# First adaLN scale in quarters, and the first projections by quarters of k, in a hybrid decoder step

## The chip, the core and the metric

The kernel runs on one core of one Trainium2 chip. It is one launch. The metric is the time of that launch on the device in microseconds (us), the median of several runs. The engines are TensorE (PE), VectorE (DVE), ScalarE (ACT), GpSimd (POOL) and SyncE (SP). SP issues nearly all of the loads.

## What is computed

One layer of a decoder runs over 256 prompt tokens and 8 samples of 4 tokens: 288 columns in all. What matters here is its beginning:

```python
mod = jax.nn.silu(c) @ P['w_ada'] + P['b_ada']          # 9 conditions, 2048 x 12288
sh1, sc1, gt1, sh2, sc2, gt2 = split(mod, 6)
xn = rmsnorm(x, P['g_norm1']) * (1.0 + sc1) + sh1
proj = xn @ P['w_in']                                   # 2048 x 12312
```

The parts of `proj` then feed an RG-LRU branch, a GLA branch and an mLSTM branch, whose merged output, with a gate, is added to x. A squared-ReLU MLP with its own scale and shift follows, and a last RMSNorm. All inputs are f32. The outputs are y and the branches' new states.

## The kernel before

Activations lie feature by feature: a k-tile is 128 features on the partitions by 288 columns (256 of the prompt, 32 of the samples). x has 16 k-tiles and fills two buffers, `xa` and `xb`; there are ten such buffers of eight k-tiles, `slot(0)` to `slot(9)`.

**Projections.** `stream` runs through the weights by blocks of 512 output features and, inside a block, by groups of two k-tiles. A group is one DMA of 512 KB into `raw`; ACT rounds it to `hi` (L156), DVE makes the rest `lo` (L157). Each matmul of f32 precision is three in the faster type: hi times xh (L163), hi times xl (L164), lo times xh (L165), where xh and xl are the same two parts of the activation (`split`, L431 and L432). A group is 24 matmuls. There are three buffers each of `raw`, `hi` and `lo`. A block's results leave PSUM by ACT (`to_slot`) or, if they are added to an earlier part, by DVE (`plus_slot`, L470).

**Conditioning.** `cond_product` multiplies silu(c) with one kind of `w_ada`, load by load (1 MB each), in matmuls whose output is 32 partitions wide (L256); four such column groups of PE take the four 32-feature parts of the columns. At the end `by_feature` transposes the result on DVE (L219), and `ada_finish` adds the bias (L278, L281). `units` gives the order of these loads: first scale in two halves (`sc0`, `sc`), first shift, then a correction, then the other kinds.

**The early projections.** The first three blocks (`NPRE`; the q, k and part of v) start before the shift is known: they take the scaled norm without shift, and the correction `shift_product`, shift times weights, is added later. They run over the first eight k-tiles as soon as `sc0` is there, then over the other eight. Then the shift is added to the activations (`shift`; `whole` first rebuilds them from xh and xl on POOL), and all later blocks use the full ones.

**Order.** The code gives the order of the SP queue by hand. `every` sets a pattern, one word for each weight group: L issues one conditioning load, V multiplies those that have landed. `slots` lists the buffers that conditioning loads take in turn (L, in five buffers, during the early projections). The order of the instructions on PE, ACT, DVE and POOL is made by a planner when the program is built; each engine then works through its list in that order.

## Time and profile before

| | |
|---|---|
| median of 3 runs | 2000.64 us (2000.48 to 2002.02) |
| the profiled execution | 1999.18 us, of which the profile's span is 1997.4 us |
| PE busy in the span | 1960.1 us (98%) |
| DVE, ACT, POOL busy | 1018.1, 820.3, 250.2 us |
| first projection matmul | at 38.32 us |
| end of the last product of the first shift | at 131.88 us |
| first projection matmul with shifted activations | at 143.81 us |

Times in the profile count from the start of the span. A row of a group gives the line, the engine, the operation, the output and inputs by the program's names, and how often it ran. In a row of the timeline or of the chain the first number is the start and the second the length. A matmul's length is modelled; the distance between two starts tells the rate. A row of waits says who waited, for whom, and then the total, the number and the longest wait. A row of a stretch gives each engine's busy time and number of instructions, then PE's granted clock (1.00 is full), the busy share of the DMA engines, and GB/s.

### The profile page before, as it was taken

To read this page: it belongs to the slowest core of one execution; us is meant where nothing else is said; L and a number is where in the kernel's file an instruction comes from. 1 tells how busy PE (TensorE), PEld (TensorE's weight loads), DVE (VectorE), ACT (ScalarE), POOL (GpSimd) and SP (SyncE) were. 2 spreads that over 40 slices of the span, in tenths; PEclk is the share of its full clock that TensorE was granted. 3 is DMA by queue.
4 is the path that set the end of the run, shared out by engine and by line. 5 is a ranking of instruction groups with operands and counts; after the bars stand their busy time and mean duration, and the time that the engine had idled before them with its cause. 6 is when DMAs were issued, how large, how long until landed. Compare 5 with 4: busy or idle time off the path is not lost.

```text
span 1997.4 us, 35369 instructions
## 1 busy us (share of the span) xinstructions
PE 1960.1 (98%) x14830; PEld 1839.4 (92%) x14830; DVE 1018.1 (51%) x1496; ACT 820.3 (41%) x1153; POOL 250.2 (13%) x330
## 2 busy tenths in 40 slices
PE   6999999999999999999999999999999999999997
PEld 4879888998899998899999989999999999999997
DVE  3453556545673456554444564334454545444565
ACT  3333465535454344343333454443343434343433
POOL 0300200001124021200112331000000101010101
PEclk8999999999999999999999999999999999999999
DMA  9988755647644358967779646654445444444443
GB/s 373 399 331 289 284 211 220 243 149 245 201 152 137 124 174 261 311 219 267 265 274 353 249 134 225 221 201 159 158 166 174 166 161 159 171 167 169 159 159 121
DMA packets 119472, 429.56 MB, mean 215 GB/s; under 512 B 11760, under 2 KB 11920, under 8 KB 119184
## 3 DMA queue, kind: packets, MB, share of 16 engines
q1 hardware_dynamic: 109744, 392.56, 54.9%
q0 software_dynamic: 7984, 28.99, 4.3%
q10 hardware_dynamic: 1584, 5.75, 0.8%
q8 instruction: 116, 1.90, 0.4%
q14 instruction: 44, 0.36, 0.1%
HBM read 410.44 MB, written 16.81 MB: 214 GB/s over the span
## 4 chain that ended last, share of the span: by engine, by line
PE 93%; DMA 4%; DVE 2%; issue 0%; ACT 0%; POOL 0%; DVEq 0%; ACTq 0%; SPq 0%; POOLq 0%
PE mm L163 28%; PE mm L165 27%; PE mm L164 27%; PE pa L256 5%; DMA s<-wada 1%; DMA o_C_s<-st 1%; DVE s L537 1%; DMA s<-x 1%; DVE lo L157 0%; DMA st<-mC 0%; PE px L586 0%; PE px L817 0%; DMA o_C_s<-s 0%; PE px L1197 0%; PE pi L1262 0%
## 5 line engine op out<-in xcount | busy, mean ns | idle before, releaser
L157 DVE TENSOR_TENSOR lo<-raw,hi 128x1024 fp32r<-128x1024 f32 x450 | 558.2, 1242 | 611.8 <-ACT hi L156 583.2
L156 ACT ACTIVATE hi<-raw 128x1024 fp32r<-128x1024 f32 x450 | 476.8, 1060 | 833.9 <-PE mm L164 601.1
L163 PE MATMUL mm<-xh,hi 128*128 128x288 f32 x2576 | 763.6, 300 | 6.8 <-ACT xh L431 4.6
L164 PE MATMUL mm<-xl,hi 128*128 128x288 f32 x2576 | 758.7, 297 | 0.0
L165 PE MATMUL mm<-xh,lo 128*128 128x288 f32 x2576 | 738.5, 296 | 1.7 <-DVE lo L157 1.7
L163 PEld LDWEIGHTS mm<-xh,hi 128*128 128x128 f32 x2576 | 483.8, 189 | 32.4 <-issue 14.5
L163 PE MATMUL mm<-s,hi 128*128 128x288 f32 x1664 | 490.6, 297 | 0.1
L164 PE MATMUL mm<-s,hi 128*128 128x288 f32 x1664 | 488.6, 295 | 0.0
L164 PEld LDWEIGHTS mm<-xl,hi 128*128 128x128 f32 x2576 | 486.1, 189 | 2.2 <-issue 0.5
L165 PEld LDWEIGHTS mm<-xh,lo 128*128 128x128 f32 x2576 | 478.9, 189 | 4.3 <-DVE lo L157 2.3
L165 PE MATMUL mm<-s,lo 128*128 128x288 f32 x1664 | 476.7, 295 | 0.4 <-DVE lo L157 0.4
L163 PEld LDWEIGHTS mm<-s,hi 128*128 128x128 f32 x1664 | 311.8, 188 | 5.7 <-issue 4.2
L164 PEld LDWEIGHTS mm<-s,hi 128*128 128x128 f32 x1664 | 312.5, 188 | 0.8 <-issue 0.5
L165 PEld LDWEIGHTS mm<-s,lo 128*128 128x128 f32 x1664 | 308.4, 188 | 2.1 <-issue 1.3
L157 DVE TENSOR_TENSOR lo<-s,hi 128x1024 fp32r<-128x1024 f32 x80 | 98.0, 1225 | 114.9 <-ACT hi L156 114.9
L156 ACT ACTIVATE hi<-s 128x1024 fp32r<-128x1024 f32 x80 | 84.9, 1062 | 142.8 <-PE mm L164 142.1
L1446 POOL TENSOR_TENSOR t<-t 128x288 f32<-128x288 f32 x64 | 60.2, 951 | 645.0 <-ACT t L1445 645.0
L256 PE MATMUL pa<-s,silc 128*32 128x512 f32 (+1 forms) x496 | 54.3, 523 | 6.0 <-DMA s<-wada 6.0
L1462 DVE TENSOR_TENSOR s<-s,mm 128x288 f32<-128x288 f32 x96 | 40.3, 450 | 33.9 <-PE mm L165 32.6
L969 POOL TENSOR_TENSOR s<-s,t 128x288 f32<-128x288 f32 x32 | 29.5, 948 | 193.4 <-DVE t L968 193.4
L432 DVE TENSOR_TENSOR s<-t,s 128x288 fp32r<-128x288 f32 x64 | 33.8, 568 | 15.6 <-ACT s L431 15.6
L256 PEld LDWEIGHTS pa<-s,silc 128*32 128x32 f32 x496 | 14.6, 112 | 27.1 <-issue 14.5
(379 smaller groups left out, 1148.2 us busy)
## 6 DMA issues: line engine op xcount, KB each, us to landing
raw<-win SPq DMA_DIRECT2D x192, 512.0 KB, 4.8
raw<-wf SPq DMA_DIRECT2D x176, 512.0 KB, 4.2
s<-wada SPq DMA_DIRECT2D x49, 1024.0 KB, 9.0
s<-wf SPq DMA_DIRECT2D x80, 512.0 KB, 3.5
ag<-wada SPq DMA_DIRECT2D x29, 1024.0 KB, 5.8
raw<-wout SPq DMA_DIRECT2D x32, 512.0 KB, 6.1
st<-wada SPq DMA_DIRECT2D x24, 512.0 KB, 6.9
s<-win SPq DMA_DIRECT2D x14, 768.0 KB, 6.6
```

What stands on the lines that cost most here:

```text
L156: pace["hi"] = S.activation(hi, raw, AF.Copy)
L157: pace["lo"] = V.tensor_tensor(out=lo, in0=raw, in1=hi.bitcast(F32), op=ALU.subtract)
L163: T.matmul(pss[m][:, :N], hi[:, kk, ms], xh, start=k == k0, stop=False)
L164: T.matmul(pss[m][:, :N], hi[:, kk, ms], xl, start=False, stop=False)
L165: pace["last"] = T.matmul(pss[m][:, :N], lo[:, kk, ms], xh, start=False, stop=k == kt - 1)
L256: pace["prod"] = T.matmul(ps[32 * j:32 * j + 32, h * w // 4:(h + 1) * w // 4], stat(k), v[:, j], start=k == 0 and h == 0, stop=k == KT - 1 ...
L432: V.tensor_tensor(out=dst_l[:, r], in0=src[:, r], in1=dst_h[:, r].bitcast(F32), op=ALU.subtract)
L537: V.scalar_tensor_tensor(y[:, m, s:NP], x[:, m, 0:NP - s], w[:, m, j:j + 1], y[:, m, s:NP], ALU.mult, ALU.add)
L969: G.tensor_tensor(out=a, in0=a, in1=t, op=ALU.add)
L1446: G.tensor_tensor(out=r, in0=r, in1=r, op=ALU.mult)
L1462: V.tensor_tensor(out=a, in0=a, in1=p, op=ALU.add)
```

## The change

- x is loaded on SP's queue right behind the conditions; before, it came on ACT's queue. The `eye` constants come early, the rest of the constants later.
- The squares of x are made by ACT and DVE in turn and summed in four column groups of PE; x is multiplied by the norm at once, in place.
- The first scale comes in quarters of 512 columns (four k-tiles of the activation). The first quarter goes through `cond_product`. The others (`ada_quarter`) give each of PE's four column groups another k-tile and all 512 columns, so that four partial sums arise; two copies on ACT and eight small matmuls with `eye` add and transpose them.
- The early projections run by quarters of k: three blocks over four k-tiles each, four times. The results of the second to fourth quarter are added on DVE. The first weight group is loaded and converted ahead (`fetch`), before the last load of the first quarter.
- Loads of the second and third quarter and the first of the shift are mixed by hand; eight buffers take them in turn.
- `modulate` scales or shifts x in place, on DVE alone; POOL's part and `whole` are gone. The shift of k-tiles 0 to 11 is applied when the shift's product ends, which is before the last early block; that of 12 to 15 after it.

```diff
...
         at["n"] += 1
         return [weight_tile(n) for n in ("raw", "hi", "lo")]
+    fetched = []
+    def fetch(w, blk, g, kg=2, ahead=True):
+        with tc.high_priority() if ahead else nullcontext():
+            raw, hi, lo = (t.rearrange("p (k m) -> p k m", k=kg) for t in weight_tiles())
+            Q.dma_start(raw, w[blk, g].rearrange("p (k m) -> p k m", k=kg))
+            pace["hi"] = S.activation(hi, raw, AF.Copy)
+            pace["lo"] = V.tensor_tensor(out=lo, in0=raw, in1=hi.bitcast(F32), op=ALU.subtract)
+        return hi, lo
     def stream(w, blk, act, kt, evac, g0=0, width=512, ahead=True, k0=0, kg=2):
         nm_t = width // P
         pss = [pm.tile([P, 512], F32, tag="mm", name=nm("mm")) for _ in range(nm_t)]
         for g in range(k0 // kg, kt // kg):
-            with tc.high_priority() if ahead else nullcontext():
-                raw, hi, lo = (t.rearrange("p (k m) -> p k m", k=kg) for t in weight_tiles())
-                Q.dma_start(raw, w[blk, g0 + g].rearrange("p (k m) -> p k m", k=kg))
-                pace["hi"] = S.activation(hi, raw, AF.Copy)
-                pace["lo"] = V.tensor_tensor(out=lo, in0=raw, in1=hi.bitcast(F32), op=ALU.subtract)
+            hi, lo = fetched.pop(0) if fetched else fetch(w, blk, g0 + g, kg, ahead)
             for m in range(nm_t):
                 for kk in range(kg):
                     k = kg * g + kk
...
             if next(g, side) is side:
                 side.remove(g)
+    def halves(a, b):
+        return lambda k: a[:, k, :] if k < 8 else b[:, k - 8, :]
     ct, th9 = (t288()[:, 0:KT * 9].rearrange("p (k c) -> p k c", k=KT) for _ in range(2))
     Q.dma_start(ct, io["ct"])
+    xa, xb = slot(0), slot(1)
+    xin = halves(xa, xb)
+    for i in range(4):
+        Q.dma_start((xa, xb)[i // 2][:, 4 * (i % 2):4 * (i % 2) + 4, :], io["x"][:, 4 * i:4 * i + 4, :])
+    a, w = COFF["eye"]
+    G.dma_start(con[:, a:a + w], io["con"][:, a:a + w])
     S.activation(th9, ct, AF.Tanh, scale=0.5)
+    S.activation(sc([P, 1], "warm", 1), th9[:, 0, 0:1], AF.Sqrt, bias=eps, scale=0.0)
     V.scalar_tensor_tensor(th9, th9, 1.0, ct, ALU.add, ALU.mult)
     silc = cp.tile([P, KT * 9 + 23], F32, tag="silc", name="silc")
     V.memset(silc[:, KT * 9:], 0.0)
...
             return [sp.tile([P, 1028], F32, tag="st", name=nm("st"), bufs=2)[:, 0:1024] for _ in range(2)]
         return [flat(slot(i))[:, 0:2048]]
-    def cond_product(name, load, each, cols, stat, finish):
+    def cond_product(name, load, each, cols, stat, finish, bank=None):
         acc_ = []
         def products(raw, q):
             if not acc_:
-                acc_.append(pa.tile([P, 512], F32, tag="pa", name=nm("pa")))
+                acc_.append(bank() if bank else pa.tile([P, 512], F32, tag="pa", name=nm("pa")))
             ps = acc_[0]
             w = cols // len(raw)
             for i in range(each):
...
         def end():
             hs = range(-(-cols // 1024))
-            with tc.high_priority():
-                pvs = [by_feature(acc_[0], h, min(256, cols // 4 - 256 * h)) for h in hs]
             for h in hs:
                 with tc.high_priority():
-                    finish(h, pvs[h])
+                    finish(h, by_feature(acc_[0], h, min(256, cols // 4 - 256 * h)))
         n = KT // each
         for q in range(n):
...
                     Q.dma_start(raw[h], wada[kind, h, k])
             else:
                 Q.dma_start(raw[0].rearrange("p (h m) -> p h m", h=2), wada[kind, :, k].rearrange("h p m -> p h m"))
+        def first_shift(h, pv):
+            ada_finish(kind)(h, pv)
+            for q in ((0, 1), (2,))[h]:
+                modulate(4 * q, ALU.add, kind, 2 if q else 1)
+        if kind == SH1:
+            return cond_product(kind, load, 1, 2048, silu_c, first_shift, longp)
         return cond_product(kind, load, 1, 2048, silu_c, ada_finish(kind))
-    def ada_half(name, kind, h):
+    def first_quarter(kind):
         def load(raw, q):
-            Q.dma_start(raw[0].rearrange("p (k m) -> p k m", k=2), wada[kind, h, 2 * q:2 * q + 2].rearrange("k p m -> p k m"))
-        return cond_product(name, load, 2, 1024, silu_c, lambda _, pv: ada_finish(kind)(h, pv))
+            Q.dma_start(raw[0].rearrange("p (k m) -> p k m", k=4), wada[kind, 0, 4 * q:4 * q + 4, :, 0:512].rearrange("k p m -> p k m"))
+        return cond_product("sc0", load, 4, 512, silu_c, ada_finish(kind))
+    def ada_quarter(kind, i):
+        acc_ = []
+        c0 = 512 * (i % 2)
+        def products(raw, q):
+            if not acc_:
+                acc_.append(pa.tile([P, 512], F32, tag="pa", name=nm("pa")))
+            n = 4 // len(raw)
+            for j in range(4):
+                pace["prod"] = T.matmul(acc_[0][32 * j:32 * j + 32, :], silu_c(4 * q + j), raw[j // n][:, 512 * (j % n):512 * (j % n) + 512],
+                                        start=q == 0, stop=q == 3, skip_group_check=True)
+        def end():
+            p = misc()
+            for h in range(2):
+                t = t288()[:, 0:256]
+                S.copy(t, acc_[0][:, 256 * h:256 * h + 256])
+                for m in range(2):
+                    a = NS * (2 * h + m)
+                    T.matmul(p[:, a:a + NS], t[:, m * P:(m + 1) * P], eye, start=True, stop=True)
+            ada_finish(kind, 4 * i)(0, p[:, 0:4 * NS].rearrange("p (m c) -> p m c", c=NS))
+        for q in range(4):
+            def ld(q=q):
+                raw = raw_tile()
+                n = 4 // len(raw)
+                for h, r in enumerate(raw):
+                    k = 4 * q + n * h
+                    Q.dma_start(r.rearrange("p (k m) -> p k m", k=n), wada[kind, i // 2, k:k + n, :, c0:c0 + 512].rearrange("k p m -> p k m"))
+                return raw
+            yield f"sc{i}", ld, lambda raw, q=q: products(raw, q), end if q == 3 else None
     def shift_product(dst, nb):
...
     shifts = []
     def units():
-        yield from ada_half("sc0", SC1, 0)
-        yield from ada_half("sc", SC1, 1)
-        yield from ada(SH1)
+        yield from first_quarter(SC1)
+        q1, q2, q3 = (ada_quarter(SC1, i) for i in (1, 2, 3))
+        sh1 = ada(SH1)
+        for g in (q1, q1, q1, q1, sh1, q2, q2, q2, q2, sh1, sh1, sh1, q3, q3, q3, q3):
+            yield next(g)
+        yield from sh1
         yield from shift_product((qk, vv), NPRE)
         for k in (GT1, SH2, SC2, GT2):
             yield from ada(k)
...
     def smp(a):
         return a[..., NP:N].rearrange("p k (b t) -> p k b t", b=NB)
-    def modulate(xg, rs, k0, fk, xh, xl, xr):
-        V.tensor_tensor(out=xr, in0=xg, in1=rs.unsqueeze(1).to_broadcast([P, 4, N]), op=ALU.mult)
-        bc = [P, 2, NB, TS]
-        for j in range(0, 4, 2):
-            r = slice(k0 + j, k0 + j + 2)
-            for i in range(j, j + 2):
-                V.tensor_scalar(xr[:, i, 0:NP], xr[:, i, 0:NP], mod[:, fk, k0 + i, 0:1], None, ALU.mult)
-            xs = smp(xr[:, j:j + 2])
-            G.tensor_tensor(out=xs, in0=xs, in1=mod[:, fk, r, 1:9].unsqueeze(3).to_broadcast(bc), op=ALU.mult)
-            split(xh[:, r, :], xl[:, r, :], xr[:, j:j + 2])
-    def whole(k0, xh, xl, xr):
-        G.tensor_tensor(out=xr, in0=xh[:, k0:k0 + 4, :].bitcast(F32), in1=xl[:, k0:k0 + 4, :].bitcast(F32), op=ALU.add)
-    def shift(k0, shk, xh, xl, xr):
-        for j in range(0, 4, 2):
-            r = slice(k0 + j, k0 + j + 2)
-            for i in range(j, j + 2):
-                V.tensor_scalar(xr[:, i, 0:NP], xr[:, i, 0:NP], mod[:, shk, k0 + i, 0:1], None, ALU.add)
-            xs = smp(xr[:, j:j + 2])
-            V.tensor_tensor(out=xs, in0=xs, in1=mod[:, shk, r, 1:9].unsqueeze(3).to_broadcast([P, 2, NB, TS]), op=ALU.add)
-            split(xh[:, r, :], xl[:, r, :], xr[:, j:j + 2])
+    def modulate(k0, op, kind, step=2):
+        x = (xa, xb)[k0 // 8][:, k0 % 8:k0 % 8 + 4, :]
+        for j in range(0, 4, step):
+            r = slice(k0 + j, k0 + j + step)
+            for i in range(j, j + step):
+                V.tensor_scalar(x[:, i, 0:NP], x[:, i, 0:NP], mod[:, kind, k0 + i, 0:1], None, op)
+            xs = smp(x[:, j:j + step])
+            V.tensor_tensor(out=xs, in0=xs, in1=mod[:, kind, r, 1:9].unsqueeze(3).to_broadcast([P, step, NB, TS]), op=op)
+            split(xh[:, r, :], xl[:, r, :], x[:, j:j + step])
     def split(dst_h, dst_l, src):
         n = src.shape[1]
...
             S.activation(dst_h[:, r], src[:, r], AF.Copy)
             V.tensor_tensor(out=dst_l[:, r], in0=src[:, r], in1=dst_h[:, r].bitcast(F32), op=ALU.subtract)
-    def halves(a, b):
-        return lambda k: a[:, k, :] if k < 8 else b[:, k - 8, :]
-    xa, xb = slot(0), slot(1)
-    xin = halves(xa, xb)
-    for i in range(4):
-        t = (xa, xb)[i // 2]
-        S.dma_start(t[:, 4 * (i % 2):4 * (i % 2) + 4, :], io["x"][:, 4 * i:4 * i + 4, :])
     xh = big.tile([P, KT, N], F32R, tag="xh", name="xh1")
     xl = big.tile([P, KT, N], F32R, tag="xl", name="xl1")
     ps = longp()
     for k in range(KT):
         sq = t288()
-        S.activation(sq, xin(k), AF.Square)
-        T.matmul(ps[:, :N], ones, sq, start=k == 0, stop=k == KT - 1)
-    rs = rstd_of(ps)
+        if k % 2:
+            V.tensor_tensor(out=sq, in0=xin(k), in1=xin(k), op=ALU.mult)
+        else:
+            S.activation(sq, xin(k), AF.Square)
+        r = slice(32 * (k % 4), 32 * (k % 4) + 32)
+        T.matmul(ps[r, :N], ones[:, 0:32], sq, start=k < 4, stop=k >= KT - 4, skip_group_check=True)
+    t = t288()
+    S.copy(t, ps[:, :N])
+    ps = misc()
+    T.matmul(ps[:, :N], ones, t, start=True, stop=True)
+    rs = inv_sqrt(row("lf"), ps[:, :N], bias=eps, scale=1.0 / (32 * D))
+    for k in range(0, KT, 4):
+        t = (xa, xb)[k // 8][:, k % 8:k % 8 + 4, :]
+        V.tensor_tensor(out=t, in0=t, in1=rs.unsqueeze(1).to_broadcast([P, 4, N]), op=ALU.mult)
     def act1(k):
         return xh[:, k, :], xl[:, k, :]
...
         return f
-    slots["ids"] = 2, 4, 5, 6, 7, 8, 9, None
-    drain("sc0")
-    xs3, xs4 = slot(3), slot(4)
+    slots.update(ids=(8, 9, 3, 4), n=0)
+    for i in range(4):
+        if i == 3:
+            fetched.append(fetch(win, B_Q, 0))
+        load_one()
+    for i in range(4):
+        visit(1)
     qk, vv = slot(8), slot(9)
     def plus_slot(dst, base):
...
             V.tensor_tensor(out=dst[:, base + m, :], in0=dst[:, base + m, :], in1=p, op=ALU.add)
         return f
-    def scale1(h):
-        t = (xa, xb)[h]
-        for i in range(2):
-            with tc.high_priority():
-                modulate(t[:, 4 * i:4 * i + 4, :], rs, 8 * h + 4 * i, SC1, xh, xl, (xs3, xs4)[i % 2][:, 0:4, :])
-    slots["ids"] = 2, 5, 6, 7, None
-    scale1(0)
-    G.tensor_copy(con[:, 0:1], mod[:, SC1, 0, 0:1])
-    G.dma_start(con, io["con"])
-    every("L LV " * 4 + "L LLV L LV " * 3 + "LV" + " ." * 40)
-    for b in range(NPRE):
-        run(stream(win, B_Q + b, act1, 8, to_slot((qk, vv)[b // 2], 4 * (b % 2))))
-    drain("sc")
-    scale1(1)
-    for b in range(NPRE):
-        run(stream(win, B_Q + b, act1, KT, plus_slot((qk, vv)[b // 2], 4 * (b % 2)), k0=8))
-    xrs = [(xs3, xs4)[i % 2][:, 4 * (i // 2):4 * (i // 2) + 4, :] for i in range(4)]
-    for i in range(4):
-        whole(4 * i, xh, xl, xrs[i])
-    drain(SH1)
+    slots.update(ids=(2, 5, 6, 7, None, "st", 3, 4), n=0)
+    every("LL LL . V L LLV  LL L LV L L LV  LL L LV L LL LV  LL L LV LL . .")
+    for q in range(4):
+        assert f"sc{q}" in done
+        with tc.high_priority():
+            modulate(4 * q, ALU.mult, SC1, 2 if q else 1)
+        if q == 0:
+            a, w = COFF["eye"]
+            for r in (slice(0, a), slice(a + w, CW)):
+                G.tensor_copy(con[:, r.start:r.start + 1], mod[:, SC1, 0, 0:1])
+                G.dma_start(con[:, r], io["con"][:, r])
+        for b in range(NPRE):
+            if q == 3 and b == NPRE - 1:
+                drain(SH1)
+            to = plus_slot if q else to_slot
+            run(stream(win, B_Q + b, act1, 4 * q + 4, to((qk, vv)[b // 2], 4 * (b % 2)), k0=4 * q))
     with tc.high_priority():
-        for i in range(4):
-            shift(4 * i, SH1, xh, xl, xrs[i])
+        modulate(12, ALU.add, SH1)
     every("L L L L . V")
-    slots.update(ids=(5, 6, 7, None, 0, 1, 3, 4), n=0)
+    slots.update(ids=(3, 4, None, 5, 0, 1, 6, 7), n=0)
     for b in range(NPRE, 4):
         run(stream(win, B_Q + b, act1, KT, to_slot((qk, vv)[b // 2], 4 * (b % 2))))
     lx = slot(2)
```

More of the change, by code (lines that the diff above doesn't have):

```diff
@@ L273, in cond_product, with ada_finish @@
             yield name, ld, lambda raw, q=q: products(raw, q), end if q == n - 1 else None
-    def ada_finish(kind):
+    def ada_finish(kind, k0=0):
         def finish(h, pv):
-            o = mod[:, kind, 8 * h:8 * h + 8, :]
-            V.tensor_tensor(out=o, in0=pv[:, :, 0:9], in1=bada[:, kind, 8 * h:8 * h + 8].unsqueeze(2).to_broadcast([P, 8, 9]), op=ALU.add)
+            n = pv.shape[1]
+            r = slice(k0 + 8 * h, k0 + 8 * h + n)
+            o = mod[:, kind, r, :]
+            V.tensor_tensor(out=o, in0=pv[:, :, 0:9], in1=bada[:, kind, r].unsqueeze(2).to_broadcast([P, n, 9]), op=ALU.add)
             if kind in (SC1, SC2):
                 gg = Pm("g1" if kind == SC1 else "g2")
-                V.scalar_tensor_tensor(o, o, 1.0, gg[:, 8 * h:8 * h + 8].unsqueeze(2).to_broadcast([P, 8, 9]), ALU.add, ALU.mult)
+                V.scalar_tensor_tensor(o, o, 1.0, gg[:, r].unsqueeze(2).to_broadcast([P, n, 9]), ALU.add, ALU.mult)
         return finish
```

## Prediction

> **What bounds the kernel now.** I read the page first, then what TensorE (PE) waited for, then the stretches around those waits, then the chain of waits there.
>
> ```profile
> span 1997.4 us, 35369 instructions
> PE 1960.1 (98%) x14830; PEld 1839.4 (92%) x14830; DVE 1018.1 (51%) x1496; ACT 820.3 (41%) x1153; POOL 250.2 (13%) x330
> ...
> PE mm L163 <- ACT xh L431: 4.6, 1, 4.6
> PE mm L163 <- DVE s L470: 2.2, 1, 2.2
> PE mm L165 <- DVE lo L157: 2.1, 3, 1.1
> ```
>
> PE is the bound: 98% busy, so a microsecond counts only where PE has none of its matmuls to do. The change touches the start, where the idle time is. In the stretches the columns are PE, weight loads, DVE, ACT, POOL, granted clock, DMA share, GB/s.
>
> ```profile
> 0.00:20.41 20.41, 13.29 (x81) 7.98 (x81) 2.17 (x9) 8.98 (x20) 1.79 (x11) 1.00 0.93 359
> 20.41:38.32 17.91, 7.95 (x81) 2.63 (x81) 6.83 (x15) 2.37 (x4) 2.00 (x6) 0.65 0.93 366
> 42.80:131.88 89.08, 89.08 (x746) 72.21 (x744) 37.87 (x45) 28.74 (x37) 16.33 (x8) 1.00 0.97 382
> 141.62:143.81 2.19, 0.01 (x1) 0.03 (x1) 2.19 (x6) 1.24 (x2) 0.00 (x0) 1.00 1.05 410
> 145.20:148.60 3.40, 3.40 (x17) 3.40 (x16) 3.40 (x7) 0.20 (x1) 0.00 (x0) 0.50 0.81 278
> 148.60:154.90 6.30, 6.30 (x49) 6.30 (x49) 4.54 (x5) 2.50 (x3) 0.00 (x0) 1.00 0.35 106
> ```
>
> Projections start at 38.32. From 42.80 to 131.88 PE and DMA are both full. Then come a gap of 2.19 and a window of 3.40 at half clock. Now the chain at the first start, and the two loads that pin the data's arrival:
>
> ```profile
> 20.41 1.07 PE L256 MATMUL pa<-s,silc 128*32 128x256 f32 x16 [0.91 <-DMA s<-wada]
> 31.80 1.94 PE L256 MATMUL pa<-s,silc 128*32 128x256 f32 x16 [0.62 <-DMA s<-wada]
> ...
> 34.17 1.18 DVE lo L157
> 35.80 1.12 DVE s L407 x3
> 37.00 1.27 ACT xh L431 x2
> 38.32 1.33 PE mm L163 x4
> ```
>
> The eighth load of the first scale (1.05 MB each) lands at 31.80; its product, transpose, scaling and the split into xh take 6.5 to 38.32. At the other end, the first shift (timeline; the last row is the chain's):
>
> ```profile
> 130.82 1.06 PE L256 MATMUL pa<-s,silc 128*32 128x512 f32 x8
> 131.95 0.78 DVE L219 STREAM_TRANSPOSE t<-pa 128x256 f32<-128x256 f32 x2 [3.53 <-PE pa L256]
> 132.66 1.18 DVE L157 TENSOR_TENSOR lo<-raw,hi 128x1024 fp32r<-128x1024 f32 x1
> 134.05 1.23 DVE L157 TENSOR_TENSOR lo<-raw,hi 128x1024 fp32r<-128x1024 f32 x1
> 135.18 0.62 DVE L421 TENSOR_SCALAR s<-s,mod 128x256 f32<-128x256 f32 x2
> 135.71 0.23 DVE L423 TENSOR_TENSOR s<-s,mod 128x64 f32<-128x64 f32 x1
> 143.81 0.37 PE mm L163
> ```
>
> I call the end of the shift's last product E: 131.88 here. DVE then shifts, and PE starts the next block at 143.81.
>
> **Part 1, the start.** Only a quarter of the first scale (4 loads) instead of a half (8) precedes the first projection. The conditions, x (2.36 MB), parameters (0.28) and constants add 2.73 MB, one weight load 0.52: 7.45 MB. By 20.41 before had moved 359 GB/s x 20.41 = 7.33 MB, though the fourth load needed only 6.9: loads behind it took 0.4. At 31.80 that lag is 0.9 (7.33 + 11.39 x 0.41 = 12.0 against 11.1). I take 0.65. The quarter reads rows of 2 KB, not 4 KB; the trace's only 2 KB reads come with the correction's loads:
>
> ```profile
> DMA packets 1646, 4.00 MB, mean 400 GB/s; under 512 B 97, under 2 KB 97, under 8 KB 1645
> 160.00:170.00 10.00, 10.00 (x88) 8.06 (x87) 2.98 (x3) 2.12 (x2) 0.00 (x0) 1.00 1.04 400
> ```
>
> About 1549 packets for 3.98 MB means 59% of the bytes in 2 KB packets, at 400 GB/s against 410 for 4 KB alone; so 2 KB alone runs near 393, and 4.2 MB cost 0.4 more. The Trainium skill, "DMA: Bandwidth & Descriptors", section "Why small descriptors are slow (HBM only)", gives a fixed overhead of about 3 cycles a packet on 32-byte beats; that is an estimated 2.3% for 2 KB against 4 KB, where the row gives 4%. By the rule the eight early quarter loads would cost 0.4 less than I count.
>
> The quarter is there at 20.41 + (7.45 + 0.65 - 7.33)/0.41 + 0.4 = 22.7. Its product takes up to 1.94, then the 4.5 from 33.78 to 38.32 without the conversion in between (1.18) and with one k-tile instead of four ahead of xh (0.8): projections start near 27, 11 earlier.
> ```profile
> 0.73 2.45 ACTq L442 DMA_DIRECT2D s<-x  x4
> L402 DVE TENSOR_TENSOR s<-s,row 128x1152 f32<-128x1152 f32 x2 | 2.6, 1346 | 0.0
> ```
>
> x's four DMAs leave ACT's queue for SP's, ahead of the quarter loads: about 2.45 of issuing that pushes the first load's issue back, and 2.36 MB counted above. x is then complete near 9.5, the squares (now half on ACT, half on DVE, in packed matmuls) near 12, and the four multiplications by the norm (1.35 each, all before the split now) near 19. The cover is the loading until 22.7: nothing, as long as x comes less than 3 late; without it up to 5.4 would lie on the path. The earlier table load and the shift's product in another PSUM bank hold nobody up: ACT and that bank are idle by then.
>
> **Part 2, the second block.** The queue order of the changed program puts all four loads of the second quarter ahead of the second block's first weights. To there it needs 8 quarter loads (8.39 MB), 3 weight loads (1.57), the 2.73 and the late constants (0.30): 13.0 MB. Landing: 20.41 + (13.0 + 0.65 - 7.33)/0.41 + 0.9 = 36.7; conversion on ACT next.
>
> ```profile
> L156 ACT ACTIVATE hi<-raw 128x1024 fp32r<-128x1024 f32 x11 | 11.5, 1058 | 19.3 <-PE mm L164 11.9 <-DMA raw<-win 4.7 <-PE mm L165 2.8
> 151.37 0.29 PE L163 MATMUL mm<-xh,hi 128*128 128x288 f32 x1
> 151.50 0.29 PE L164 MATMUL mm<-xl,hi 128*128 128x288 f32 x1
> 145.41 0.44 PE L163 MATMUL mm<-xh,hi 128*128 128x288 f32 x1
> 145.65 0.44 PE L164 MATMUL mm<-xl,hi 128*128 128x288 f32 x1
> 47.19 1.86 PE pa L256 x32
> 80.97 2.71 PE pa L256 x24
> 83.69 0.33 PE mm L163
> 648.34 1.87 PE L1151 MATMUL px<-s,s 128*128 128x32 f32 x16
> ```
>
> So the second block starts at A = 36.7 + 1.06 + 0.1 = 37.9. The first block (48 matmuls, 0.133 apart, or 0.24 at half clock) from 27 ends at 34 to 36: PE waits 2 to 4 here.
>
> **Part 3, A to E.** PE's order is fixed by the program. From A to the shift's last product it holds 20 weight groups of 24 matmuls at 0.133: 64.0. Twelve quarter loads at 0.93 (1.86/2): 11.1; sixteen shift loads at 0.90 (2.71/3): 14.5. Eight returns to projections at 0.2 (0.33 less 0.133): 1.6. The k-tile-per-column-group form adds two ACT copies and 8 small f32 matmuls per quarter for three quarters; 16 of such a shape took 1.87, so with the switch 1.1 each: 3.3. The copies are covered by the 10 to 23 matmuls ahead of the small ones. Nine blocks instead of three are now evicted by adds on DVE; in its order, at two block changes without products between, the next lo stands behind four adds, and PE, with 8 matmuls in hand, waits about 0.7 each: 1.4 (ends: 0 and nine times 0.7). The sample parts of the scale move from POOL to DVE, which has the room (37.87 of 89.08). SP's queue waits for a product or a conversion before most loads, as before, but with eight buffers instead of five the DMA engines keep work: by bytes (32 loads of wada, 22 weight loads, 3.0 MB of the rest: 48.1 MB) the last shift load lands at 20.41 + (48.1 + 0.65 - 7.33)/0.41 + 1.8 = 123, so DMA doesn't set E. E = 37.9 + 64.0 + 25.6 + 1.6 + 3.3 + 1.4 = 133.8, against 131.88.
>
> The four additions on POOL that rebuilt x vanish at no gain: they lay inside the full stretch (POOL 16.33 there).
>
> **Part 4, after E.** DVE's costs:
>
> ```profile
> 124.10 2.05 DVE L470 TENSOR_TENSOR s<-s,mm 128x288 f32<-128x288 f32 x4 [3.70 <-PE mm L165]
> 149.35 1.43 DVE L432 TENSOR_TENSOR xl<-s,xh 128x576 fp32r<-128x576 f32 x2
> ```
>
> The changed DVE order has the same transposes, two conversions and two additions of bias: first shift at E + 3.3 (135.18 less 131.88). Then, before xl of the third k-tile, stand 16 shifts (0.265), 9 sample adds (0.13), 4 block adds (0.45), 2 conversions (1.18), 4 double xl (0.67) and 3 single ones (0.4, estimated as half and a start): 13.4. The order finishes k-tiles 8 to 15 before the third. PE has two groups left after E (6.4), then 16 matmuls, and waits: for the second k-tile near E + 13, the third at E + 16.7. Its 72nd matmul of the next block ends at E + 22.8. Before, 72 from 143.81 (10 at 0.133, 14 at 0.24, 48 at 0.133) end at 154.9 = E + 23.0. So the shift is no faster. Before's 2.19 gap already brought 3.40 at half clock; with some 5 idle of 7 here I add one window more behind the gap: 14 matmuls instead of 25, 1.5 (ends: 0 and 3).
>
> **The sum.** 133.8 + 22.8 + 1.5 = 158.1 against 154.9: +3.2. Behind it every engine's order is that of before and PE is full, so it goes through. The profiled execution took 1999.18 (span 1997.4 and 1.8 around it), 1.5 under the median; it would read 2002.4, and the median 2000.64 + 3.2 = 2003.8.
>
> **Rivals.** 0.2% (4.0) is about what can be told from no change.
>
> *Half clock twice* (slower). PE's wait ahead of A is about as long as the 2.19 gap. If it also halves the clock, 1.5 more between A and E: 2005.3. For it: the 0.50 row, and 0.65 from 20.41 to 38.32. Against: a wait under 2 decides otherwise. The Trainium skill, "TensorE: Matmul & The Clock Gate", section "What's actually happening", has the clock halved after an idle window of about 3.4 us and freed after a busy one; its windows run free, so a 2-4 us wait may or may not do it, and the 0.50 row agrees with the window's length.
>
> *Adds ahead of conversions* (slower). If all nine blocks that end in adds hold up the next lo by 0.7, 4.9 more: 2008.7. It decides from two more such waits on. For it: L165 waited for lo three times before. Against: products cover most block changes.
>
> *Data in time* (no change). Lag 0.4, no 2 KB cost, constants later: landing at 34.5, A = 35.7, E = 130.2 without lo waits, no more half clock: 153.0, -1.9, so 1998.7.
>
> *Early start kept* (faster). Data in time, and the 2.1 for which PE waited on lo further down also goes: 1996.6 or less. PE's own work from 27 to E leaves hardly more; E can't fall much below 128.5.
>
> That projections don't start earlier at all would need the quarter loads at half speed; I give that nothing.
>
> **How the numbers follow.** My sum 0.43 (own range 2001 to 2006, of which 0.13 lies over 2004.6), half clock 0.20, adds 0.13, data in time 0.10, early start kept 0.14. Faster 0.14; same 0.30 + 0.10 = 0.40; slower 0.13 + 0.20 + 0.13 = 0.46. The range leaves a tenth at each end: 1997.5 to 2009.5.
>
> **What would show it.** First projection near 27; a PE wait of 2 to 4 for hi at the second block; shift's last product ending near 134; DVE unbroken for 17 behind it and PE waiting twice. An E under 130, or PE going on within 3 of its last early block, would prove me wrong.

## The result: slower by 0.29%, and the profile after

The changed kernel takes 2005.44 us (median of 13 runs, 2002.33 to 2008.51) against 1999.83 for the kernel before on the same chip: a ratio of 1.0029, 95% interval 1.0020 to 1.0037, or 5.7 us more. The profiled execution took 2004.7, with a span of 2002.9 against 1997.4.

From the page of the changed kernel, the busy times:

```profile
PE 1960.5 (98%) x14832; PEld 1840.0 (92%) x14832; DVE 1032.9 (52%) x1547; ACT 820.3 (41%) x1157; POOL 229.4 (11%) x321
```

PE is as busy as before (1960.5 against 1960.1), so by this count 5.1 of the 5.5 more of span are idle time of PE; work at half clock counts as busy. Its timeline of the changed kernel (start, duration, operation, in brackets what it waited for; xh, hi and xl are the rounded and remainder tiles):

```profile
24.02 1.94 PE L273 MATMUL pa<-s,silc 128*32 128x128 f32 x32 [4.05 <-DMA s<-wada]
27.82 1.33 PE L170 MATMUL mm<-xh,hi 128*128 128x288 f32 x4 [1.87 <-ACT xh L476]
39.34 0.40 PE L170 MATMUL mm<-xh,hi 128*128 128x288 f32 x1 [2.19 <-ACT hi L155]
134.72 1.92 PE L273 MATMUL pi<-s,silc 128*32 128x512 f32 x16
149.11 0.40 PE L171 MATMUL mm<-xl,hi 128*128 128x288 f32 x1 [2.44 <-DVE xl L477]
152.87 0.61 PE L171 MATMUL mm<-xl,hi 128*128 128x288 f32 x1 [1.09 <-DVE xl L477]
...
160.39 0.29 PE L172 MATMUL mm<-xh,lo 128*128 128x288 f32 x1
```

Projections start at 27.82, 10.5 earlier than before. The second block starts at A = 39.34, after a wait of 2.19 for its weights. The shift's last product ends at E = 134.72 + 1.92 = 136.64, 4.8 later than before. Behind it PE waits three times more: 0.57 at 143.77 for the first shifted k-tile, then 2.44 and 1.09 for xl from DVE. The last row is the 72nd matmul of the next block, whose place the prediction summed up to (154.9 before, 160.5 now). The stretches around these places (columns as in the prediction):

```profile
27.82:36.99 9.17, 9.17 (x48) 9.04 (x48) 3.31 (x9) 3.27 (x7) 0.63 (x2) 0.67 1.04 392
36.99:39.34 2.35, 0.16 (x3) 0.01 (x1) 0.03 (x1) 1.52 (x3) 0.00 (x0) 1.00 1.03 413
40.60:44.10 3.50, 3.50 (x16) 3.50 (x16) 2.45 (x2) 1.09 (x2) 0.00 (x0) 0.51 0.81 281
44.10:136.64 92.54, 90.97 (x716) 70.45 (x715) 44.13 (x80) 29.03 (x40) 0.00 (x0) 1.00 0.98 375
143.77:149.11 5.34, 2.87 (x17) 2.24 (x17) 5.34 (x14) 2.55 (x5) 0.00 (x0) 1.00 1.04 393
149.11:152.87 3.76, 2.67 (x12) 2.32 (x12) 3.76 (x9) 1.63 (x2) 0.00 (x0) 0.60 0.27 106
152.87:156.00 3.13, 3.13 (x13) 3.13 (x14) 2.92 (x5) 0.69 (x1) 0.00 (x0) 0.50 0.54 168
```

Three things cost here: the gap at 37 to 39; a window at half clock that begins 1.3 after it (16 matmuls in 3.50, where a full clock gives 26); and behind E a stretch in which DVE is busy without a break while PE is not, with the clock at 0.50 to 0.60.

### The profile page after: what moved, and what is told of

It is laid out like the page before. It is cut to its first block, busy times and chain, and to the rows that moved or that the text cites. A ratio compares the mean times of both kernels' runs of the same rounds, so it can differ in the third digit from the quotient of the medians.

```text
span 2002.9 us, 35426 instructions
## 1 busy us (share of the span) xinstructions
PE 1960.5 (98%) x14832; PEld 1840.0 (92%) x14832; DVE 1032.9 (52%) x1547; ACT 820.3 (41%) x1157; POOL 229.4 (11%) x321
## 4 chain that ended last, share of the span: by engine, by line
PE 93%; DVE 2%; DMA 2%; SPq 1%; issue 0%; ACT 0%; POOL 0%; DVEq 0%; ACTq 0%; POOLq 0%
PE mm L170 28%; PE mm L172 27%; PE mm L171 27%; PE pa L273 3%; DMA raw<-win 1%; PE pi L273 1%; DVE lo L156 1%; PE pa L338 1%; SPq L357 0%; PE pi L1308 0%; PE px L1316 0%; PE px L632 0%; PE px L863 0%; DVE s L371 0%; DMA raw<-wbm 0%
## 5 line engine op out<-in xcount | busy, mean ns | idle before, releaser
L476 ACT ACTIVATE s<-t 128x288 fp32r<-128x288 f32 x64 | 28.0, 441 | 24.6 <-POOL t L1492 24.6
L273 PE MATMUL pa<-s,silc 128*32 128x512 f32 (+1 forms) x312 | 31.7, 479 | 6.5 <-DMA s<-wada 6.5
```

Of the source, the lines that this page charges most:

```text
L273: pace["prod"] = T.matmul(ps[32 * j:32 * j + 32, h * w // 4:(h + 1) * w // 4], stat(k), v[:, j], start=k == 0 and h == 0, stop=k == KT - 1 ...
L476: S.activation(dst_h[:, r], src[:, r], AF.Copy)
```

## The experiments

All times are compared with runs of the kernel before on the same chip. E is the end of the shift's last product in each kernel's profile. The table is for finding one's way; the readings follow.

| kernel | E, us | median, us | ratio to before, 95% interval |
|---|---|---|---|
| before | 131.88 | 1999.8 | 1 |
| changed | 136.64 | 2005.4 | 1.0029, 1.0020 to 1.0037 |
| weights_first | 132.57 | 1999.9 | 1.0003, 0.9994 to 1.0012 |
| gap_filled | 135.36 | 2004.5 | 1.0023, 1.0013 to 1.0032 |
| x_on_act_queue | 135.07 | 2002.7 | 1.0014, 1.0005 to 1.0023 |
| old_form | 134.86 | 2000.5 | 1.0004, 0.9995 to 1.0013 |
| five_buffers | 147.64 | 2018.5 | 1.0095, 1.0081 to 1.0108 |
| shift_early | 130.53 | 2001.8 | 1.0011, 1.0003 to 1.0020 |
| shift_in_order | 136.93 | 1997.5 | 0.9995, 0.9986 to 1.0004 |
| before_shift_in_order | 131.69 | 1995.6 | 0.9980, 0.9972 to 0.9989 |
| first_and_third | 131.76 | 1994.8 | 0.9985, 0.9976 to 0.9994 |
| three_mended | 130.23 | 1993.5 | 0.9968, 0.9955 to 0.9980 |
| three_mended_again | 130.28 | 1991.8 | 0.9964, 0.9951 to 0.9978 |
| clock_kept_up | 131.22 | 1994.7 | 0.9984, 0.9976 to 0.9993 |

### The second block's weights first

```diff
-    every("LL LL . V L LLV  LL L LV ...
+    every("LL . . LLV L LLV  LL L LV ...
```

> The changed kernel, with two of the second quarter's four loads queued behind the second block's weights instead of ahead of them. Theory (PE is the pace, and each wait and each half-clock window lies on the path): the wait of 2.2 for hi at the second block goes, and with it the half-clock window at 40.6 to 44.1 (another 1.6), so E moves from 136.6 to about 132.9 and the time from 2005.4 to about 2001.7. Rival (DMA, 0.98 busy from 44 to 137, is the pace): the wait only moves to the quarter's products or to later weights, E stays near 136 and the time near 2005. Third case: the wait goes and the window stays, E 134.4.

E fell by 4.1 and the ratio by 0.0026, or 5.2 us. The second block no longer waits: PE's timeline shows no wait between the first projection (27.67) and 59.73, and two stretches show it busy throughout, from 40 on at full clock:

```profile
59.73 0.40 PE L170 MATMUL mm<-xh,hi 128*128 128x288 f32 x1 [0.24 <-ACT hi L155]
```

```profile
30.00:40.00 10.00, 10.00 (x72) 10.00 (x71) 3.68 (x3) 4.46 (x7) 0.00 (x0) 0.92 1.04 393
40.00:50.00 10.00, 10.00 (x83) 7.20 (x82) 2.45 (x2) 4.05 (x8) 0.00 (x0) 1.00 1.04 393
```

The wait did not move to the quarter's products: the next one is 0.24, at 59.73. So with DMA full, the order in which the same bytes come was worth 4.1 us at E. The span of the profiled execution is 5.7 shorter (1997.2 against 2002.9); the other 1.6 came behind E, where this execution had DVE's waits as before but no half clock after them (the last section shows the rows). That part is not the order's doing.

### The same gap, filled

```diff
...
+            if q == 0 and b == 0:
+                p = misc()
+                with tc.issue_after(pace["last"].ins):
+                    for i in range(14):
+                        T.matmul(p[:, :N], last_hi[0][:, 1, 0:P], xh[:, 3, :], start=i == 0, stop=i == 13)
```

> The changed kernel with 14 extra matmuls (their sum is used by nothing) right behind the first block, where PE waits 2.2 for hi; nothing else is moved. If that wait is what halves the clock at 40.6 to 44.1, the second block still starts near 39.3, but the window is at full clock, E moves to about 135.0 and the time to about 2003.8. If the window comes from something else, the window stays, and E stays at 136.6 and the time at 2005.4 or a little over.

PE's timeline, then the stretch that was at half clock:

```profile
36.55 2.03 PE L549 MATMUL px<-xh,hi 128*128 128x288 f32 x14
39.27 0.40 PE L173 MATMUL mm<-xh,hi 128*128 128x288 f32 x1 [0.70 <-ACT hi L155]
```

```profile
40.60:44.10 3.50, 3.50 (x27) 3.50 (x28) 2.45 (x2) 1.06 (x1) 0.00 (x0) 1.00 0.90 280
```

The second block starts at the same place (39.27), but the window holds 27 matmuls instead of 16, and E falls by 1.28. So the gap cost twice: its own length, and 1.2 to 1.5 by the clock (from the second block to E 96.09 instead of 97.30, and 11 more matmuls at 0.133 in the window). That this reaches the end of the kernel is not shown: the two intervals overlap, and the span is only 0.2 shorter (2002.7).

### x on ACT's queue

```diff
-        Q.dma_start((xa, xb)[i // 2][:, 4 * (i % 2):4 * (i % 2) + 4, :], io["x"][:, 4 * i:4 * i + 4, :])
+        S.dma_start((xa, xb)[i // 2][:, 4 * (i % 2):4 * (i % 2) + 4, :], io["x"][:, 4 * i:4 * i + 4, :])
```

> The changed kernel with x's four loads issued from ACT's queue, as before the change, instead of first on SP's. Theory (x's place is worth nothing, since the norm is done before the first quarter of the scale is): projections start at 27.8 or up to 1 later, the time is within 1 of 2005.4. Rival (the queue matters): SP issues the scale's loads 2.5 earlier and the start moves forward by 1 or more, or x comes behind the scale's loads, the norm is late and the start moves back by 2 or more.

Both expectations missed. Projections start 1.3 later, which is the sign of the second half of the rival, and yet the time is 3.0 lower.

```profile
29.10 1.33 PE L170 MATMUL mm<-xh,hi 128*128 128x288 f32 x4 [3.91 <-ACT xh L476]
38.99 0.40 PE L170 MATMUL mm<-xh,hi 128*128 128x288 f32 x1 [0.86 <-ACT hi L155]
```

```profile
40.00:50.00 10.00, 10.00 (x80) 7.03 (x79) 3.79 (x4) 4.63 (x9) 0.00 (x0) 1.00 0.91 313
```

The second block's weights came 0.35 earlier; a start 1.3 later therefore left a gap of 0.86 instead of 2.19, and behind it the clock stayed at 1.00. E is 1.57 lower: 0.35 from the landing, and 136.64 - 39.34 - (135.07 - 38.99) = 1.2 from the clock. The spans of the profiled executions differ by 1.4 (2001.5 and 2002.9), so what is gained at E accounts for all of it there. The 3.0 come from the two ratios, whose intervals overlap, and are no safer than that. The start of the projections was not what E hung on: the second block's data were.

### The quarters in the first quarter's form

```diff
...
-        q1, q2, q3 = (ada_quarter(SC1, i) for i in (1, 2, 3))
+        q1, q2, q3 = (first_quarter(SC1, i) for i in (1, 2, 3))
...
-    slots.update(ids=(2, 5, 6, 7, None, "st", 3, 4), n=0)
+    slots.update(ids=(2, 5, 6, 7, None, 3, 4), n=0)
```

> The changed kernel with quarters two to four of the first scale in the form of its first quarter (128-column matmuls, transposed by DVE) instead of one k-tile per column group and sums through the identity; the two half-size buffers are left out of the turn (seven instead of eight). Theory (PE is the pace): a load costs 1.94 instead of 0.91, so a quarter costs 7.8 instead of 3.6 + 1.0: E is 9.4 later, near 146, and the time near 2015. Rival (DMA is the pace between A and E): most of the 9.4 is hidden, and the time rises by 3 or less.

Both missed in sign: E fell by 1.8, though the second block waited 0.85 longer than in the changed kernel.

```profile
39.30 0.61 PE L170 MATMUL mm<-xh,hi 128*128 128x288 f32 x1 [3.04 <-ACT hi L155]
48.62 3.70 PE L273 MATMUL pa<-s,silc 128*32 128x128 f32 x128
```

```profile
39.30:45.30 6.00, 6.00 (x25) 6.00 (x26) 3.65 (x3) 2.11 (x2) 0.00 (x0) 0.50 0.91 327
```

In the changed kernel, from its timeline, from its groups of 44 to 137, and the same 6 us:

```profile
47.63 3.64 PE L338 MATMUL pa<-s,silc 128*32 128x512 f32 x32
```

```profile
L348 PE MATMUL px<-con,t 128*128 128x32 f32 x24 | 2.9, 265 | 0.0
```

```profile
39.34:45.34 6.00, 6.00 (x32) 5.83 (x33) 3.65 (x3) 2.12 (x2) 0.00 (x0) 0.72 0.89 322
```

Four loads in the old form took 3.70, 0.93 each. I had read 1.94 a load from the row at 24.02, where PE had just idled 4.05 and the clock was low (0.68 from 20 to 30). At full clock the two forms cost about the same (3.64 against 3.70 for four loads), and the new one's sums through the identity come on top: 24 matmuls of 2.9 in all. Nearly all of that came back here. The longer wait itself cost nothing, since the first block ended earlier and the second starts in the same place (39.30 against 39.34). From there to E it takes 95.56 instead of 97.30, 1.7 less, although the half clock lasted longer: the rows of 6 us hold 25 matmuls instead of 32, another 0.9. The time fell by 5.0, more than E. The profiled execution is the longest of the 11, and its span (2002.8) is that of the changed kernel, so what the 5.0 consists of is not seen.

### Five buffers

```diff
-    slots.update(ids=(2, 5, 6, 7, None, "st", 3, 4), n=0)
+    slots.update(ids=(2, 5, 6, 7, None), n=0)
```

> The changed kernel with five buffers in turn for the modulation loads instead of eight (the order of issue unchanged). Theory (from A to E PE is the pace and the loads have about 10 us in hand with eight buffers): SP waits more often, the loads lose some of that lead, E moves by 0 to 2, time 2005 to 2008. Rival (the eight buffers carry the early quarters): PE waits for loads at several products, E moves by 5 or more, time 2010 or more.

The rival holds in its numbers: E moved by 11.0 and the time by 13. In the changed kernel the stretch from 40 to 50 moves 340 GB/s. The same stretch with five buffers, then SP's queue, PE's row at 68 and the sum of such waits to 180:

```profile
40.00:50.00 10.00, 10.00 (x60) 8.94 (x62) 3.64 (x4) 4.18 (x7) 0.00 (x0) 0.72 0.30 102
```

```profile
40.62 0.33 SPq L154 DMA_DIRECT2D raw<-win  x1
49.81 0.38 SPq L357 DMA_DIRECT2D s<-wada  x1
```

```profile
68.13 0.40 PE L170 MATMUL mm<-xh,hi 128*128 128x288 f32 x1 [2.25 <-ACT hi L155]
```

```profile
PE mm L170 <- ACT hi L155: 8.3, 6, 3.1
```

SP issues nothing for nine microseconds, until the quarter's products at 48 have freed a buffer, and DMA runs dry; what is late then are not the products but the weights queued behind. The lead that the prediction counted on comes from the three added buffers.

### The shift one block earlier

```diff
-    every("LL LL . V L LLV  LL L LV L L LV  LL L LV L LL LV  LL L LV LL . .")
+    every("LL LL . V L LLV  LL LV L LV LL LV  L LV LL LV LL LV  LL LV . . . .")
...
-            if q == 3 and b == NPRE - 1:
+            if q == 3 and b == NPRE - 2:
```

> The changed kernel, with the first shift's products all done one block (two groups, 6.4 us) earlier and its loads issued accordingly. Theory: E falls to about 130.5, PE then has four groups (12.8) ahead of it while DVE does its 16 us of shifting, so the three waits behind E (0.6, 2.4, 1.1) and most of the two half-clock windows (3.4 lost) go: time 1999 to 2001. Rival (data): the shift's loads cannot come 6.4 earlier, since the DMA engines are full, PE waits for them instead, and the time stays at 2005 or rises.

E came where it should (126.03 + 4.50 = 130.53, with no wait for data there), and the time fell by 3.6, somewhat less than expected. PE's and DVE's timelines:

```profile
39.02 0.61 PE L170 MATMUL mm<-xh,hi 128*128 128x288 f32 x1 [3.17 <-ACT hi L155]
103.95 0.40 PE L170 MATMUL mm<-xh,hi 128*128 128x288 f32 x1 [1.42 <-ACT hi L155]
126.03 4.50 PE L273 MATMUL pi<-s,silc 128*32 128x512 f32 x40
140.29 0.41 PE L170 MATMUL mm<-xh,hi 128*128 128x288 f32 x1 [2.17 <-ACT xh L476]
```

```profile
139.70 0.44 DVE L522 TENSOR_TENSOR s<-s,mm 128x288 f32<-128x288 f32 x1
```

The waits for weights are longer (3.17 at the second block, and a new one of 1.42), and behind E the last early block waits 2.17 with the DVE work of the shift in progress. What ended just before that block went on (139.70 + 0.44) is the first add that evicts the block before it, which DVE had put behind its shifts. That it was this add, and not the write of xh that the profile names, is inferred from the times alone.

### The shift in order

DVE's order behind E is chained: the shift of the next k-tile or pair, then the remainder xl of the one before.

```diff
-            for q in ((0, 1), (2,))[h]:
-                modulate(4 * q, ALU.add, kind, 2 if q else 1)
+            shift_chain(((0, 1), (1, 1), (2, 2), (4, 2), (6, 2)) if h == 0 else ((8, 2), (10, 2)))
...
+    def shift_chain(ks):
+        for k, n in ks:
...
+            with tc.issue_after(chain["xl"].ins) if chain["xl"] else nullcontext():
+                for i in range(n):
+                    V.tensor_scalar(x[:, i, 0:NP], x[:, i, 0:NP], mod[:, SH1, k + i, 0:1], None, ALU.add)
+                xs = smp(x)
+                last = V.tensor_tensor(out=xs, in0=xs, in1=mod[:, SH1, r, 1:9].unsqueeze(3).to_broadcast([P, n, NB, TS]), op=ALU.add)
+            if chain["at"]:
+                with tc.issue_after(last.ins):
+                    chain_xl()
+            S.activation(xh[:, r], x, AF.Copy)
...
```

> The changed kernel; behind E only the order of DVE's work is changed: shift of k-tile k+1 (or pair), then the remainder xl of k, and so on from 0 to 15, instead of twelve k-tiles shifted first. Theory (the three waits behind E come from DVE's order, not its amount): a k-tile costs DVE 0.75 of shifting and splitting and 0.6 of weights' remainder, less than PE's 1.6, so E stays near 136.6, the waits behind E (4.1 in all) fall to about 1, the half-clock windows at 149 to 156 go (3.4), and the time falls by 6 to 7 to about 1999. Rival (the amount of DVE work is what counts): the waits are only spread, and the time falls by less than 2.

E stayed (136.93) and the time fell by 6.8. The stretch behind E, where DVE is as busy as before (18.13 of 19.07):

```profile
136.93:156.00 19.07, 19.03 (x143) 18.67 (x142) 18.13 (x46) 10.18 (x14) 0.00 (x0) 1.00 0.78 271
```

PE does 143 matmuls with next to no wait and at full clock. The same DVE work in another order takes nothing from PE. The changed kernel had shifted the prompt columns of all sixteen k-tiles, the last two at 150.71, before it made xl of the third; its DVE rows:

```profile
150.71 0.61 DVE L466 TENSOR_SCALAR s<-s,mod 128x256 f32<-128x256 f32 x2
152.37 0.45 DVE L477 TENSOR_TENSOR xl<-s,xh 128x288 fp32r<-128x288 f32 x1
```

The kernel before had a fault of the same kind in the same place, though there PE waited for another piece of DVE's work (the wait of 2.19 for L470 that the prediction shows): the first add that evicts the last early block, which DVE did behind its shifts.

> The kernel before the change, with DVE's shift of k-tiles 0 to 15 put in the same order as in shift_in_order (shift of the next pair, then the remainder of the last). Theory (before loses 2.2 by the wait at 141.6 and 1.6 by the half-clock window behind it to the same order of DVE's work): both go, time lower by 3 to 4, near 1995.5; E stays at 131.9. Rival (before's wait comes from something else than the order): less than 1.

With the chain it takes 0.9980 of the kernel before, 4.0 less, and neither the gap of 2.19 at 141.62 nor the window at 145.20 is left:

```profile
140.00:150.00 10.00, 10.00 (x77) 10.00 (x76) 10.00 (x23) 5.45 (x8) 0.00 (x0) 1.00 0.94 349
```

The chain brings that add forward as well. Here it is on DVE before, and then with the chain, where it has line 491:

```profile
143.22 0.45 DVE L470 TENSOR_TENSOR s<-s,mm 128x288 f32<-128x288 f32 x1
```

```profile
139.25 0.45 DVE L491 TENSOR_TENSOR s<-s,mm 128x288 f32<-128x288 f32 x1
```

### Together

> The changed kernel with the second block's weights queued ahead, the quarters in the first quarter's form, and the shift in order, together. Theory (the three losses lie one behind the other on PE's path): 5.5 and 5 less by the medians measured for the first two, 6 to 7 less for the third: time near 1989, E near 130.5. Rival (they overlap, since the loads of the first shift bound E from below): E stays over 131 with PE waiting for DMA, time 1993 to 1996.

> three_mended without its change of form: quarters two to four with one k-tile per column group and sums through the identity, as in the changed kernel; the second block's weights ahead and the shift in order. Theory (the form costs its sums, three times 1.2, on PE's path): E 132.6 as in weights_first, time 3 over three_mended, near 1996.5. Rival (with the other two mended the form is hidden): the same time as three_mended, 1993.5.

> three_mended once more, since its first comparison rests on five runs. If the early start is worth something beside a shift in order, the ratio to the kernel before lies at 0.9965 to 0.9975, under the 0.998 of before_shift_in_order; if it is worth nothing, at 0.998 or over.

The first comparison of the three met its theory at E (130.23) and its rival in time (1993.5); without the form, E lies between theory and rival. The three edits together take 12.6 from the changed kernel (0.9966, the mean of the two comparisons, against 1.0029). Singly they took 5.2, 5.0 and 6.8, 17.0 in all, so by these figures they overlap by about a quarter. A part of the overlap is seen: 1.6 of what the first gained in its profile lay behind E, in the half clock that the third takes away. Without the change of form the other two give 8.8 of their 12.0. The form is worth 1.5 at E there (131.76 against 130.23), and some 4 in time. Both comparisons of the three (0.9968, 0.9964) lie under the before that has the shift in order (0.9980), by about 3 us, with intervals that overlap. So this version is faster than the changed kernel and the kernel before, but that the early start adds to the order of the shift is likely and not certain, and over half of its gain on the kernel before is the order of DVE's shift, which the early start has nothing to do with.

Then the half clock at the very start, by extra matmuls in PE's idle time ahead of the first projection:

```diff
...
         visit(1)
+        if i >= 2:
+            n = (8, 6)[i - 2]
+            p = misc()
+            with tc.issue_after(pace["prod"].ins):
+                for j in range(n):
+                    T.matmul(p[:, 0:P], ones, ones, start=j == 0, stop=j == n - 1)
```

> three_mended with 14 extra matmuls (their sums are used by nothing) in TensorE's two idle stretches ahead of the first projection, 8 while it waits for the quarter's fourth load and 6 while x is scaled and split. Theory (the first block runs at half clock because PE idles before it): the first 48 matmuls take 6.5 instead of 9, E moves from 130.2 to about 128, and the time falls by 2 from three_mended's 1993.4. Rival (behind the first block the loads set the pace): PE waits for weights at the second or third block instead, E within 0.7 of 130.2, time the same.

The rival comes nearer, but not where it was expected. The stretch 20 to 30 goes to a clock of 0.83 (0.54 in three_mended) and 30 to 40 to 1.00 (0.94). The first projection starts 0.2 later (28.03 against 27.80), and a new wait for weights stands late, at 118.80, and not at the second or third block:

```profile
25.90 2.38 PE L544 MATMUL px<-ones 128*128 128x128 f32 x12
118.80 0.40 PE L170 MATMUL mm<-xh,hi 128*128 128x288 f32 x1 [1.42 <-ACT hi L155]
```

E is 1.0 later than in three_mended and the time no lower. This profile is of the longest of the 11 runs. The matmuls seem to run into the loads: from 20 to 120 DMA is full here (1.03 to 1.04). The two profiles of the three edits say the same. From 30 to 40 one has a clock of 0.94 with 73 matmuls, the other 0.81 with 64, and yet E lies at 130.23 and 130.28. So with the three edits in, data and PE look level, and a faster first block gives no more; why the load at 118.80 came later is not shown.

## Why the prediction came out

The forecast was 2003.8 and the time 2005.4. The sum was +3.2, the spans differ by 5.5. Its direction and its places were right; the 2.3 that it lacks lie in two steps. That the time came within 1.6 is in part luck: the kernel before took 1999.83 in this comparison, 0.8 less than the 2000.64 on which the forecast stood. By the prediction's own limit of 4.0 its sum meant no clear change, and the 5.7 measured are a slower kernel, to which it gave 0.46 in all.

*Part 1* had the projections near 27 (27.82) and the quarter there at 22.7 (24.02). That is where the first miss begins: the sum took before's 359 GB/s for the first 20 us, and here it is 340:

```profile
0.00:20.00 20.00, 10.19 (x130) 4.85 (x130) 9.22 (x20) 7.11 (x14) 2.34 (x12) 1.00 0.92 340
20.00:30.00 10.00, 4.12 (x41) 3.51 (x42) 6.18 (x17) 2.64 (x5) 1.48 (x4) 0.68 1.04 387
```

0.019 MB/us over 20 us are 0.38 MB, 0.9 at 0.41. A part of that is the price of 2 KB rows, for which the sum had 0.4 already, so not all of the 1.3 is traced. The 387 of the next stretch is nearer to the 393 that the row at 160 gave for 2 KB packets than to the 410 of 4 KB, so the row's 4% is not too much. From the overhead of about 3 cycles a packet in the Trainium skill, "DMA: Bandwidth & Descriptors", section "Why small descriptors are slow (HBM only)", the estimate was 2.3%, too little by these rows; but nothing here parts the packets' size from the traffic beside it.

That x's place costs nothing failed. Its cover (the norm done before the quarter is there) did hold, but that was not all it touched: on ACT's queue E comes 1.57 earlier, and the time is 3.0 lower by ratios whose intervals overlap.

*Part 2* had A at 37.9; it was 39.34, by the same late data. The wait of 2 to 4 was 2.19, and weights_first shows that the queue order made it.

*Part 3* gave 95.9 from A to E and 97.3 were measured. PE's waits of the changed kernel up to 165:

```profile
PE mm L170 <- ACT hi L155: 2.2, 1, 2.2
...
PE mm L172 <- DVE lo L156: 1.6, 3, 0.6
```

The terms held: a quarter load 0.91 (3.64/4) for 0.93, a quarter's sums 0.97 (2.9/3) for 1.1 with the switch, the waits for lo 1.6 in all, three of them, for 1.4. The 1.4 left is the half-clock window, to which the prediction gave 0.20 as a rival of its own, at 1.5 and 2005.3. So the likeliest case was wrong on this term, and the rival it had written for that term is what happened; gap_filled shows it. The rival's condition (a wait about as long as the 2.19 gap) was met to the hundredth, but that such a wait halves the clock was partly luck, as the last section shows. The other slower rival, adds ahead of all conversions, did not come: it spoke of nine such waits and was to decide from two more than the sum's two, and there were three. "DMA doesn't set E" held by virtue of the eight buffers, as five_buffers shows.

*Part 4* had the first shift at E + 3.3 (139.94, so 3.3), xl of the third k-tile at E + 16.7 (152.37, so 15.7) and the 72nd matmul at E + 24.3 with the extra half clock; it ends at 160.5, E + 23.9. This step was right, 0.4 too high. It named DVE's order (k-tiles 8 to 15 finished before the third) but took it as given, and the 17 us of DVE work as the limit; shift_in_order does the same work in another order with next to no wait of PE.

In sum: landing +1.4, clock +1.4, behind E -0.4: 2.4, where the spans ask for 2.3.

## What to carry to other kernels

An earlier start is worth only what the second piece of work can keep: look at which load the second block waits for, and at its place in the queue, before counting the microseconds of the first. A gap of PE costs its length and perhaps the clock behind it, so a gap that a later start would close can be cheaper than the start. Where an engine is busy without a break while another waits for it, try its order before its amount.

## What the runs showed of the hardware

The clock fell after gaps shorter than the window it fell for. In the changed kernel a gap of 2.19 brought 3.4 at half clock, and one of 2.44 a clock of 0.60; gaps of 0.70 (gap_filled) and 0.86 (x_on_act_queue) brought none. But gaps of 2.42 and 1.91 brought none either, in weights_first; its rows:

```profile
145.03 0.40 PE L171 MATMUL mm<-xl,hi 128*128 128x288 f32 x1 [2.42 <-DVE xl L477]
148.80 0.40 PE L171 MATMUL mm<-xl,hi 128*128 128x288 f32 x1 [1.91 <-DVE xl L477]
```

The Trainium skill, "TensorE: Matmul & The Clock Gate", section "What's actually happening", has windows of about 3.4 us that run free of the kernel, and a throttled clock after at least one idle window. The clock records of these traces agree with such windows: between the first change and the last, every stretch of one clock lasts a whole multiple of 3.413 us. So each trace's own changes give its windows. Below are, in the changed kernel, the window ahead of the half clock at 40.61 (the 2.19 gap lies inside it), and in weights_first two that no half clock followed (the 2.42 gap lies across both):

```profile
37.20:40.61 3.41, 1.27 (x9) 1.11 (x9) 1.23 (x1) 2.48 (x3) 0.00 (x0) 1.00 1.03 410
```

```profile
140.74:144.15 3.41, 1.88 (x14) 1.65 (x13) 3.41 (x9) 1.83 (x3) 0.00 (x0) 1.00 1.04 399
144.15:147.57 3.42, 1.86 (x12) 1.63 (x12) 3.42 (x9) 1.50 (x3) 0.00 (x0) 1.00 0.58 225
```

PE was busy for 0.37 of the first and for 0.55 and 0.54 of the others. The same holds in the 14 traces, each from 27 to 200 us. All 13 windows at full clock with PE busy for 0.46 or less were followed by half clock. Of the 46 with PE busy for 0.54 to 0.85, all but one were followed by full clock (old_form, 0.65 at 141.09; PE's busy time is modelled). So about half a window of idle time was enough here, and not a whole one as that section of the Trainium skill has it. The half clock came with the next window, in the changed kernel 1.3 after work had resumed, and an equal gap that was split between two windows did no harm. None of these kernels was built to test this.
